# Shifting every operand by 192 bytes and staggering the split-weight buffers modulo 256 bytes

## The chip, the cores and the metric

The kernel runs on one core of one Trainium2 chip. The metric is the device time of one launch in microseconds. Three timed runs of the kernel before gave 2461.67 us in the median (2457.89 to 2467.87). One further execution was profiled; it took 2464.19 us by the same clock, of which 2462.4 us lie between its first and its last instruction (the span).

## What is computed

Two layers of a diffusion backbone over 256 latent tokens (and 256 context tokens in the first layer), model width 2048, feed-forward width 5632, all in float32. Cut to what matters here, with `h` the latent tokens:

```
for i in (0, 1):
    sh1, sc1, g1, sh2, sc2, g2 = ada_params(c, ada_w[i], ada_b[i])       # 6 x 2048 numbers
    a = modulate(h, sh1, sc1)                                            # h * (1 + scale) + shift
    y = na_mixer(a, ac, ...) if i == 0 else spatial_gating_mlp(a, ...)   # attention, then gMLP
    h = layer_norm(ALPHA * h + g1 * y, ln_g[i, 0], ln_b[i, 0])
    h = layer_norm(ALPHA * h + g2 * swiglu(modulate(h, sh2, sc2), ffn_w_in[i], ffn_w_out[i]),
                   ln_g[i, 1], ln_b[i, 1])
```

Nearly all the work is products of 256 (in layer 0's key and value projections 512) token rows with weight matrices that are read once from HBM.

## The kernel before, in words

**Products.** Every large product is made in three matmuls of type fp32r, which together stand for one float32 product: `mm3` (lines 87 to 90) multiplies the high part of the stationary operand with the high and the low part of the moving one, and the low part of the stationary one with the high part of the moving one. So each operand exists twice in SBUF, as a high and a low buffer. Each matmul has its own weight load (PEld in the profile). In the profile a group is named `out<-moving,stationary`: in `pod<-hwd,ghd` the weight piece `hwd` streams and the activation `ghd` is held.

**Weights.** They come in pieces of 128 partitions x 1024 float32 (4096 bytes in each partition, 512 KB). `prefetch` (lines 105 to 125) takes the next piece from one list that holds the order of the whole program, loads it into one of four `raw` buffers from SyncE's DMA queue (line 110), and splits it: `split_into` (lines 92 to 94) has ScalarE copy the raw piece to the high buffer (CAST, line 93) and VectorE subtract that copy from the raw piece into the low buffer (TENSOR_TENSOR, line 94). The high and low buffers stand in two places. The *narrow* ones, tags `hiA` and `loA`, three each in the pool `outer`, are used by all pieces of the attention part and by three of every five pieces afterwards. The *wide* ones, tags `hiB` and `loB`, two each in the pool `main`, take the other two of five (line 118). The last piece of each product goes to an `extra` tile.

**Activations.** In attention the modulated tokens are `ah` and `al`; in the feed-forward input products they are `f0h`/`f0l` (layer 0) and `f1h`/`f1l` (layer 1), in gMLP `m1h`/`m1l`. The feed-forward output product splits its activations as it goes, into `gh`/`gl` tiles of 256 columns (`ghd`, `gld`).

**Stages**, in us of the profiled span: 0 to 160 the first three heads' keys and values, with the first modulation computed beside them (`ap` tiles: dot products on TensorE, line 350, or on VectorE, line 337); to 660 attention and its output product; to 1165 the feed-forward input of layer 0 (`pg`, `pu`); to 1400 its output (`pod`); to 1730 gMLP; to 2450 the second feed-forward; then the last layer norm and the store. Beside the products VectorE computes later modulations (`ad`, line 152, `gate`, line 176) from weights that ScalarE's DMA queue loads into the four `ada` buffers.

**Addresses.** Tiles are laid in SBUF in the order in which pools and tags are opened, one after the other, each at the same byte address in all 128 partitions. Each starts at a multiple of 32 bytes. Three small tiles tagged `pad` (128, 128 and 64 bytes) stand in the pools `main`, `pw` and `gm`. What matters below is an address modulo 256, called the residue. Before the change, by the built program's table of addresses, every high, low, raw, `ada`, activation and gate buffer has residue 64; the `ap`, `xt`, `tmp` and `row` tiles of the first 160 us have 224; `sg`, `zs`, `gTb`, `w_s` and the broadcast rows have 192; `ident` has 0. Slices of these buffers start at multiples of 512 bytes, so that all 10,464 fp32r matmuls of the program read both operands from residue 64.

Of the kernel before, what the change touches and what calls it, by code (L numbers as in the profile page):

```python
# [11 lines left out]
F32 = mybir.dt.float32  # L12
F32R = mybir.dt.float32r
# [6 lines left out]
P = 128  # L20
# [21 lines left out]
FETCH = 3  # L42
BUSY = 0.3
DVE0 = 3
W0 = HK0 * P + 512
EARLY = tuple((3 + 4 * g + h, h, 4 * g) for g in range(3) for h in range(4))
EN = 4
# [4 lines left out]
def hybrid_kernel(ctx: ExitStack, tc: tile.TileContext, i, out):  # L52
# [3 lines left out]
    outer = ctx.enter_context(tc.tile_pool(name="outer", bufs=1))  # L56
# [10 lines left out]
    S.activation(c_col, c_col, AF.Silu)  # L67
    for t in (SC1, SC2):
        V.tensor_scalar(badj[:, :, t, :], badj[:, :, t, :], 1.0, None, ALU.add)
    lncol = outer.tile([P, 4, 2, KT], F32, tag="lncol", name="lncol")  # L70
    cols = outer.tile([P, 2, 6, KT], F32, tag="cols", name="cols")
    cols2 = outer.tile([P, 2, 6, KT], F32, tag="cols2", name="cols2")
# [14 lines left out]
    def mm3(ps, sh, sl, mh, ml, first, last, keep=lambda ins: ins):  # L87
        keep(T.matmul(ps, sh, mh, start=first, stop=False))  # L88
        keep(T.matmul(ps, sh, ml, start=False, stop=False))  # L89
        keep(T.matmul(ps, sl, mh, start=False, stop=last))  # L90

    def split_into(hi, lo, src):
        S.copy(hi, src)  # L93
        V.tensor_tensor(lo, src, hi.bitcast(F32), ALU.subtract)  # L94
# [5 lines left out]
    def enqueue(src, name, widths=(1024, 1024), extra=False):  # L100
        off = 0
        for n, w in enumerate(widths):
            queue.append((src[:, off : off + w], f"{name}_{off}", w, n if extra else None))
            off += w

    def prefetch(k):
        while len(ready) < k and queue:
            src, name, n, at = queue.pop(0)
            raw = outer.tile([P, 1024], F32, tag="raw", name=f"r{name}", bufs=RAW)
            (pin if pos["pin"] else lambda ins: ins)(nc.sync.dma_start(raw[:, :n], src))  # L110
            if at is not None:
                hi, lo = pos["extra"][:, 2 * at, :], pos["extra"][:, 2 * at + 1, :]
                split_into(hi, lo, raw)
                ready.append((hi, lo))
                continue
            m = pos["n"]
            pos["n"] += 1
            if pos["wide"] is not None and m % 5 > 2:
                pool, tag, bufs = pos["wide"], "B", 2
            else:  # L120
                pool, tag, bufs = outer, "A", 3
            hi = pool.tile([P, 1024], F32R, tag="hi" + tag, name=f"h{name}", bufs=bufs)
            lo = pool.tile([P, 1024], F32R, tag="lo" + tag, name=f"l{name}", bufs=bufs)
            split_into(hi[:, :n], lo[:, :n], raw[:, :n])
            ready.append((hi, lo))

    def piece():
        prefetch(1)
        got = ready.pop(0)
        prefetch(pos["bufs"] - 1)  # L130
        return got

    def take(k):
        prefetch(k)
        got = ready[:k]
        del ready[:k]
        return got
# [98 lines left out]
    for kt in range(KT):  # L236
        enqueue(i["w_kv0"][kt], f"kv{kt}", (W0,))
        for at, h, k0 in EARLY:
# [38 lines left out]
    with tc.tile_pool(name="attnX", bufs=1) as px, ExitStack() as late:  # L277
# [21 lines left out]
        with tc.tile_pool(name="st", bufs=1) as st:  # L299
# [3 lines left out]
            def load_st(src, name, n):  # L303
                pool, tag, bufs = slots[n % 4]
                r = pool.tile([P, 2048], F32, tag=tag, name=name, bufs=bufs)
                pin(nc.sync.dma_start(r, src))
                return r
# [3 lines left out]
            def fetch(kt):  # L311
                for t in range(2):
                    src = i["ada_s"][kt - DVE0] if t and kt >= DVE0 else i["ada_p"][kt, t]
                    held[kt, t] = load_st(src, f"ap{kt}{t}", 2 * kt + t)
# [18 lines left out]
            def dot_dve(kt, t):  # L333
                r = held.pop((kt, t))
                junk = outer.tile([P, D], BF16, tag="ada", name=f"junk{kt}", bufs=ADA)
                for n, (o, bc) in enumerate(((junk, cc_bc), (r, c_bc))):
                    V.scalar_tensor_tensor(
                        o, r, 1.0, bc, ALU.mult, ALU.mult, accum_out=raw_c[:, kt, 1 - n : 2 - n]
                    )
                V.tensor_scalar(mod[:, 1, kt, :], raw_c[:, kt, :], badj[:, 0, SH1, kt : kt + 1], None, ALU.add)  # L340

            def dot(kt, t):
                if t and kt >= DVE0:
                    return dot_dve(kt, t)
                if t == 0:
                    dps[kt] = stp_pool.tile([P, 512], F32, tag="a", name=f"aps{kt}")
                r = held.pop((kt, t))
                for kk in range(KT):
                    g = 32 * (kk % 4)
                    pin(T.matmul(  # L350
                        dps[kt][g : g + 32, t * P : (t + 1) * P], c_pad[:, kk, :], r[:, kk * P : (kk + 1) * P],
                        start=kk < 4, stop=kk >= KT - 4, tile_position=(0, g),
                    ))

            def gather(kt):
                ps = dps.pop(kt)
                ts = 1 if kt >= DVE0 else 2
                row = st.tile([P, 2 * P], F32, tag="row", name=f"row{kt}", bufs=1)
# [30 lines left out]
            for kt in range(KT):  # L389
                hi, lo = piece()  # L390
# [6 lines left out]
                def values(b):  # L397
                    c, tb = slice(HK0 * P, W0), slice(b * P, (b + 1) * P)
                    mm3(vps[b], ah[:, kt, tb], al[:, kt, tb], hi[:, c], lo[:, c], first, last, pin)
# [33 lines left out]
                for at, h, k0 in EARLY:  # L433
                    if at == kt:
                        h += HK0
                        hi, lo = piece()
# [537 lines left out]
def lay_out(x, c, ctx, c_ctx, ada_w, ada_b, ln_g, ln_b, na_w_qkv, na_w_o, na_rpb,  # L974
# [25 lines left out]
    )  # L1000
    a["ada_s"] = np.stack([aw[0, :, SH1, kt * P : (kt + 1) * P].T for kt in range(DVE0, KT)])
    wq, wk, wv = (na_w_qkv[0][:, n * D : (n + 1) * D] for n in range(3))
    w0 = np.concatenate([wk[:, : HK0 * P], wv[:, :512]], 1)
    a["w_kv0"] = w0.reshape(KT, P, W0)

# [34 lines left out]
```

## Time and profile before

| | |
|---|---|
| median of three runs | 2461.67 us |
| profiled execution, whole / span | 2464.19 / 2462.4 us |
| TensorE matmul busy | 2388.5 us, 97% |
| VectorE busy | 1753.7 us, 71% |
| ScalarE busy | 1120.5 us, 46% |
| GpSimd busy | 110.3 us, 4% |
| from HBM | 606.46 MB, 247 GB/s over the span |
| granted TensorE clock, mean | 0.991 |

Times are microseconds unless marked ns. A matmul's duration in a row (391 ns, say) is that of its passage through the array; the next one starts before it ends, so what a stream of matmuls costs is the distance between starts. L88 is line 88 of the kernel. A row of the lines view reads: line, engine, operation, out<-in, shapes, count | busy us, mean ns of one | idle time of the engine before them and who ended it. A row of a source view gives minimum, median and maximum of one instruction's duration.

### The profile page before, as it was taken

To read this page: it belongs to the slowest core of one execution; us is meant where nothing else is said; L and a number is where in the kernel's file an instruction comes from. 1 tells how busy PE (TensorE), PEld (TensorE's weight loads), DVE (VectorE), ACT (ScalarE), POOL (GpSimd) and SP (SyncE) were. 2 spreads that over 40 slices of the span, in tenths; PEclk is the share of its full clock that TensorE was granted. 3 is DMA by queue.
4 is the path that set the end of the run, shared out by engine and by line. 5 is a ranking of instruction groups with operands and counts; after the bars stand their busy time and mean duration, and the time that the engine had idled before them with its cause. 6 is when DMAs were issued, how large, how long until landed. Compare 5 with 4: busy or idle time off the path is not lost. (4 is left out here: it accounts for less than half of the span.)

```text
span 2462.4 us, 31266 instructions
## 1 busy us (share of the span) xinstructions
PE 2388.5 (97%) x11574; PEld 1979.4 (80%) x11574; DVE 1753.7 (71%) x2158; ACT 1120.5 (46%) x1534; POOL 110.3 (4%) x54
## 2 busy tenths in 40 slices
PE   7999999999999999999999999899999999999998
PEld 5788888888788888887888778777888888888886
DVE  4878877777887777666778778778755555566666
ACT  3344434335554444443455554445544444445453
POOL 0000200000010010000000010020100000020000
PEclk9999999999999999999999999999999999999999
DMA  9978787877578888887888767766567676766563
GB/s 358 346 248 266 254 288 260 273 253 246 188 241 284 293 280 299 284 290 275 280 290 283 247 208 263 241 210 196 199 229 229 226 227 225 230 198 190 178 211 131
DMA packets 167682, 610.63 MB, mean 248 GB/s; under 512 B 19076, under 2 KB 21572, under 8 KB 163172
## 3 DMA queue, kind: packets, MB, share of 16 engines
q1 hardware_dynamic: 120888, 440.64, 53.9%
q10 hardware_dynamic: 46512, 167.96, 19.9%
q8 instruction: 90, 1.47, 0.2%
q14 instruction: 64, 0.52, 0.1%
q0 software_dynamic: 128, 0.03, 0.0%
HBM read 606.46 MB, written 2.10 MB: 247 GB/s over the span
## 5 line engine op out<-in xcount | busy, mean ns | idle before, releaser
L93 ACT CAST hwf<-rwf 128x1024 fp32r<-128x1024 f32 x320 | 336.9, 1053 | 491.2 <-PE pu L90 206.0
L94 DVE TENSOR_TENSOR lwf<-rwf,hwf 128x1024 fp32r<-128x1024 f32 x320 | 404.3, 1277 | 173.8 <-ACT hwf L93 172.8
L152 DVE SCALAR_TENSOR_TENSOR ad<-ad,c_bc 128x1024 f32<-128x1024 f32 x192 | 234.0, 1222 | 168.9 <-DMA ad<-in_ada_t 168.3
L88 PE MATMUL pod<-hwd,ghd 128*128 128x512 f32 x684 | 267.3, 391 | 3.5 <-DVE sg L815 3.5
L90 PE MATMUL pod<-hwd,gld 128*128 128x512 f32 x684 | 266.5, 390 | 0.7 <-DVE gld L94 0.7
L89 PE MATMUL pod<-lwd,ghd 128*128 128x512 f32 x684 | 266.8, 390 | 0.0
L176 DVE SCALAR_TENSOR_TENSOR gate<-ag,c_col,gate 128x1024 f32<-128x1024 f32 x128 | 164.4, 1288 | 121.1 <-DMA ag<-in_ada_g 120.8
L94 DVE TENSOR_TENSOR lwd<-rwd,hwd 128x1024 fp32r<-128x1024 f32 x172 | 211.7, 1232 | 51.3 <-ACT hwd L93 51.0
L93 ACT CAST hwd<-rwd 128x1024 fp32r<-128x1024 f32 x172 | 180.3, 1049 | 33.3 <-PE pu L90 11.5
L88 PEld LDWEIGHTS pod<-hwd,ghd 128*128 128x128 f32 x684 | 128.7, 188 | 30.5 <-DVE sg L815 4.0
L90 PEld LDWEIGHTS pod<-hwd,gld 128*128 128x128 f32 x684 | 128.7, 188 | 28.1 <-DVE gld L94 1.2
L89 PEld LDWEIGHTS pod<-lwd,ghd 128*128 128x128 f32 x684 | 128.8, 188 | 26.6
L88 PE MATMUL pg<-hwf,f1h 128*128 128x512 f32 x320 | 126.4, 395 | 0.0
L88 PE MATMUL pg<-hwf,f0h 128*128 128x512 f32 x320 | 126.4, 395 | 0.0
L90 PE MATMUL pg<-hwf,f1l 128*128 128x512 f32 x320 | 124.7, 390 | 0.0
L90 PE MATMUL pg<-hwf,f0l 128*128 128x512 f32 x320 | 124.7, 390 | 0.0
L88 PE MATMUL pu<-hwf,f0h 128*128 128x512 f32 x320 | 124.5, 389 | 0.0
L89 PE MATMUL pu<-lwf,f0h 128*128 128x512 f32 x320 | 124.5, 389 | 0.0
L90 PE MATMUL pu<-hwf,f0l 128*128 128x512 f32 x320 | 124.5, 389 | 0.0
L88 PE MATMUL pu<-hwf,f1h 128*128 128x512 f32 x320 | 124.5, 389 | 0.0
L89 PE MATMUL pu<-lwf,f1h 128*128 128x512 f32 x320 | 124.5, 389 | 0.0
L90 PE MATMUL pu<-hwf,f1l 128*128 128x512 f32 x320 | 124.5, 389 | 0.0
(338 smaller groups left out, 5345.1 us busy)
## 6 DMA issues: line engine op xcount, KB each, us to landing
rwf<-in_w_in_t SPq DMA_DIRECT2D x320, 512.0 KB
ad<-in_ada_t ACTq DMA_DIRECT2D x192, 512.0 KB
rwd<-in_w_out SPq DMA_DIRECT2D x176, 512.0 KB
ag<-in_ada_g ACTq DMA_DIRECT2D x128, 512.0 KB
rwg<-in_w_gin SPq DMA_DIRECT2D x64, 512.0 KB
ap<-in_ada_p SPq DMA_DIRECT2D x19, 1024.0 KB
rwq<-in_w_q SPq DMA_DIRECT2D x32, 512.0 KB
rwo<-in_w_o SPq DMA_DIRECT2D x32, 512.0 KB
```

What stands on the lines that cost most here:

```text
L88: keep(T.matmul(ps, sh, mh, start=first, stop=False))
L89: keep(T.matmul(ps, sh, ml, start=False, stop=False))
L90: keep(T.matmul(ps, sl, mh, start=False, stop=last))
L93: S.copy(hi, src)
L94: V.tensor_tensor(lo, src, hi.bitcast(F32), ALU.subtract)
L152: V.scalar_tensor_tensor(r, r, 1.0, c_bc[:, half * 1024 : (half + 1) * 1024], ALU.mult, ALU.mult, accum_out=o[:, nt : nt + 1],)
L176: V.scalar_tensor_tensor(g, loaded.pop(key), c_col[:, kt, 0:1], g, ALU.mult, ALU.add)
```

## The change

Two edits; the arithmetic, the tiles' contents and the engines' programs stay as they are.

- A tile of 48 float32 (192 bytes in each partition) that nothing uses is put into `outer` ahead of `lncol`. Everything that is allocated after it moves up by at least 192 bytes.
- The narrow high buffers become 1024 + 24 elements long, the narrow low buffers 1024 + 40; only the first 1024 are used. Three buffers of a tag stand one after the other, so that their starts step by 96 bytes (high) and 160 bytes (low) modulo 256. What lies behind the six narrow buffers moves by 960 bytes in all.

```diff
+STEP_HI, STEP_LO = 24, 40
...
+    outer.tile([P, 48], F32, tag="pad", name="pad_outer")
     lncol = outer.tile([P, 4, 2, KT], F32, tag="lncol", name="lncol")
...
-            hi = pool.tile([P, 1024], F32R, tag="hi" + tag, name=f"h{name}", bufs=bufs)
-            lo = pool.tile([P, 1024], F32R, tag="lo" + tag, name=f"l{name}", bufs=bufs)
+            wh, wl = (1024 + STEP_HI, 1024 + STEP_LO) if tag == "A" else (1024, 1024)
+            hi = pool.tile([P, wh], F32R, tag="hi" + tag, name=f"h{name}", bufs=bufs)[:, :1024]
+            lo = pool.tile([P, wl], F32R, tag="lo" + tag, name=f"l{name}", bufs=bufs)[:, :1024]
             split_into(hi[:, :n], lo[:, :n], raw[:, :n])
```

Residues (byte address modulo 256) by the address tables of the two built programs:

```
buffers                                            before        after
narrow high (three)                                64 64 64      0 96 192
narrow low (three)                                 64 64 64      32 192 96
wide high and low, extra, raw, ada, ah, al,
  f0h/f0l, m1h/m1l, f1h/f1l, gh/gl, kh/kl, th/tl   64            0
ap (three of its four slots), xt, tmp, row         224           160
ap (the fourth slot: the gate buffer)              64            0
sg, zs, gTb, w_s, broadcast rows                   192           128
ident                                              0             0

fp32r matmuls by residues (moving, stationary)     before        after
512 columns, equal residues                        9504          4708 (0, 0)
512 columns, unequal                               0             4796
   of these with an operand at 32 or 96            0             2727
256 columns, equal residues                        960           352 (0, 0)
256 columns, unequal                               0             608
   of these with an operand at 32 or 96            0             360
```

The order of instructions on each engine, and what each waits for, is the same row by row in both programs.

## The prediction

> **What bounds the kernel now.** I read the page's busy times first, then the busy times by stage, then single matmuls in order of time, then the waits of TensorE, and last the groups of VectorE and ScalarE by shape.
>
> ```profile
> PE 2388.5 (97%) x11574; PEld 1979.4 (80%) x11574; DVE 1753.7 (71%) x2158; ACT 1120.5 (46%) x1534; POOL 110.3 (4%) x54
> ```
>
> TensorE is busy for 2388.5 of 2462.4 us; 73.9 us are left. The same by stage (columns: length, busy us of PE, PEld, DVE, ACT, POOL, granted clock, DMA share, GB/s):
>
> ```profile
> 0.00:100.00 100.00, 84.19 (x725) 65.34 (x726) 61.08 (x84) 37.49 (x61) 5.24 (x8) 0.97 0.94 353
> 100.00:660.00 560.00, 541.47 (x3003) 463.94 (x3002) 436.27 (x633) 244.49 (x391) 15.23 (x3) 0.99 0.78 261
> 700.00:1165.00 465.00, 465.00 (x2092) 384.93 (x2090) 331.97 (x352) 197.56 (x212) 20.45 (x7) 1.00 0.85 287
> 1400.00:1730.00 330.00, 310.22 (x1355) 250.55 (x1354) 256.73 (x312) 165.84 (x237) 35.44 (x21) 0.97 0.66 220
> 1730.00:2450.00 720.00, 719.59 (x3222) 595.23 (x3221) 442.62 (x450) 326.58 (x404) 27.86 (x11) 1.00 0.65 209
> 2450.00:2463.00 13.00, 0.67 (x3) 0.21 (x2) 8.78 (x15) 0.29 (x1) 0.00 (x0) 0.63 0.31 120
> ```
>
> In the two feed-forward stages (465 and 720 us) TensorE never waits; 0.4 us are lost in 1185. All idle time lies in the first 100 us (15.8), attention (18.5), gMLP (19.8), the 13 us behind the last product, and a rest at the edges. So time can come from two places only: the distance between matmuls in a stream, or these edges.
>
> The distance, from 197 matmuls of 512 columns in a row (first and last shown) and 27 of 256 columns:
>
> ```profile
> 1199.74 0.39 PE L90 MATMUL pod<-hwd,gld 128*128 128x512 f32 x1
> ...
> 1244.17 0.39 PE L88 MATMUL pod<-hwd,ghd 128*128 128x512 f32 x1
> ```
>
> ```profile
> 165.83 0.28 PE L90 MATMUL qps<-ah,lwq 128*128 128x256 f32 x1
> ...
> 168.95 0.28 PE L89 MATMUL qps<-al,hwq 128*128 128x256 f32 x1
> ```
>
> 44.43 us / 196 = 226.7 ns, and 3.12 us / 26 = 120.0 ns. The 256 columns more cost 106.7 ns, so 512 cost 213.3, and 13.3 ns of each matmul do not depend on its width. That fixed 13.3 ns is the one part of a stream's time that addresses might touch.
>
> **The pads and the shift.** No instruction is added, removed or moved, no wait is added, and each transfer has the same size. What remains is whether an access takes another time at another address. I go through those who access SBUF.
>
> *TensorE.* Rows of single matmuls by line, minimum/median/maximum in ns:
>
> ```profile
> L88 PE MATMUL pu<-hwf,f0h x320: 389/389/389, 740.6 to 1161.6; 128*128 128x512 f32 x160
> L88 PE MATMUL pu<-hwf,f1h x320: 389/389/389, 1788.1 to 2209.2; 128*128 128x512 f32 x160
> ```
>
> In 640 matmuls none is a nanosecond longer than another, while ScalarE writes, VectorE reads and writes and the DMA queues fill other buffers at the same residue 64 all the time (DVE 71%, DMA share 0.85 in that stage). Three of five of those weight pieces stand in narrow buffers and two in wide ones, which differ in where they lie but not in residue. So the other engines' accesses cost TensorE nothing that staggering could give back: term 0.0 us. The bounds: all of the 13.3 ns goes away for the pairs that become unequal (first rival), or reads that start 32 bytes off cost more (second rival).
>
> The Trainium skill speaks against any such gain: "SBUF — State Buffer", section "Who interferes with whom", holds that only the port pair shared by VectorE and GpSimd causes contention, and that TensorE and ScalarE wait on nobody. By that rule the term would be 0.0 too, for every residue; the 640 equal durations agree with it for the other engines, but no row here shows it for TensorE's own two reads, which always stood at one residue.
>
> *VectorE.*
>
> ```profile
> L94 DVE TENSOR_TENSOR lwf<-rwf,hwf x320: 1209/1224/10147, 710.4 to 2197.6; 128x1024 fp32r<-128x1024 f32 x160
> L94 DVE TENSOR_TENSOR gld<-gTb,ghd x109: 416/423/426, 1205.5 to 2432.6; 128x256 fp32r<-128x256 f32 x109
> L94 DVE TENSOR_TENSOR al<-tmp,ah x16: 691/693/693, 15.7 to 152.7; 128x512 fp32r<-128x512 f32 x16
> L94 DVE TENSOR_TENSOR lwe<-rwe,hwe x12: 683/689/689, 42.6 to 146.1; 128x512 fp32r<-128x512 f32 x12
> L152 DVE SCALAR_TENSOR_TENSOR ad<-ad,c_bc 128x1024 f32<-128x1024 f32 x192 | 234.0, 1222 | 168.9 <-DMA ad<-in_ada_t 168.3
> L337 DVE SCALAR_TENSOR_TENSOR junk<-ap,oT x13: 2280/2282/2283, 36.9 to 143.9; 128x2048 bf16<-128x2048 f32 x13
> ```
>
> With all operands at 64, (1224 - 423) / 768 = 1.043 ns per element. L337 reads `ap` at residue 224, an odd multiple of 32 like the new 32 and 96: (2282 - 1222) / 1024 = 1.035. Its 13 instructions, six of them at 224 and seven at 64 in the gate buffer, lie within 3 ns. `al<-tmp,ah` reads at 224 and takes 4 ns more than `lwe<-rwe,hwe`, whose operands all stand at 64. So the term per split lies between -13 ns (median to minimum of `lwf`) and +4 ns. The narrow buffers take some 500 pieces, so VectorE changes by between -6.5 and +2 us over the run, under the cover of TensorE's stream in all stages without idle time: 0.0 us on the path. Without that cover, at the edges, where a twentieth of the pieces stands (some 25), it would be 0.3 us at most. The maximum of 10147 ns in the first row is a split that stood behind a GpSimd broadcast or reduction, and addresses do not change which instructions meet.
>
> *ScalarE.*
>
> ```profile
> L93 ACT CAST hwf<-rwf x320: 1037/1055/1060, 708.9 to 2196.5; 128x1024 fp32r<-128x1024 f32 x160
> L93 ACT CAST ghd<-gTb x109: 395/407/409, 1204.0 to 2431.4; 128x256 fp32r<-128x256 f32 x109
> ```
>
> (1055 - 407) / 768 = 0.844 ns per element with everything at 64 except `gTb`, which is at 192; durations spread over 23 ns. At most -18 ns a piece, hidden in the same way (ACT 46% busy): 0.0 us.
>
> *DMA.* Its targets `raw` and `ada` go from 64 to 0 modulo 256. The stage that it fills most is the first: share 0.94 at 353 GB/s, thus 376 GB/s per fully busy share, and there most bytes go to `ap` and `xt` at 224. In the stage at 0.85 and 287 GB/s, 338 per share, all go to residue 64. The stage with the odder residues is the faster one (its transfers are larger), so no handicap of a residue is to be seen. What quicker transfers could give back is bounded by TensorE's waits that a DMA ended:
>
> ```profile
> PE aps L350 <- DMA ap<-in_ada_p: 8.1, 2, 7.6
> PE pt L552 <- ACT p L542: 13.4, 7, 5.0
> PE gu L89 <- DVE lwg L94: 3.3, 1, 3.3
> PE vps L89 <- DVE lwv L94: 2.1, 2, 1.7
> ```
>
> 7.6 of the 8.1 us are the first load after the start, a latency. The longest other waits are for a softmax chain (`pt`) and for VectorE's split of a late piece (`gu`, `vps`). I take 0.0 us, with bounds of 0 and -16 us (all idle time of the first 100 us).
>
> The Trainium skill has a rule for this too: "DMA: Bandwidth & Descriptors", section "How a descriptor splits into AXI transactions", says that a transaction must start at a multiple of 256 bytes, so that a descriptor that begins elsewhere wastes beats. By its account of 32-byte beats, 4096 bytes from residue 64 would take 130 beats and from residue 0 128; my estimate from that page is 1.5% of the raw transfers, about 1 us of the stage that DMA fills. No row here separates targets at 0 from targets at 64 at this size.
>
> *Sum:* 2464.2 + 0.0 (TensorE) + 0.0 (VectorE, ScalarE) + 0.0 (DMA) = 2464 us for a profiled execution. The profiled execution stands 2.5 us above the median of 2461.67, so the forecast for the median is 2461 us, rounded. Its own range is 2449 to 2474, half a per cent to either side; half a per cent, 12.3 us, is also about what a measurement of this kernel can tell from no change.
>
> **Rivals.**
>
> *A, faster: TensorE's two reads collide when they stand at one residue.* For it: all 10,464 fp32r matmuls read both operands from residue 64, and all carry the same 13.3 ns, so the trace cannot tell a fixed cost from a collision that always happens. Against it: the loads read 512 bytes and the streams 1024 or 2048, and a collision that is paid anew as both walk on should grow with the overlap or scatter, where 640 rows show one value. After the change 4796 matmuls of 512 columns and 608 of 256 have unequal residues: 5404 x 13.3 ns = 71.9 us, thus 2392 us profiled and 2390 in the median. Chance 0.13.
>
> The Trainium skill gives this rival a figure: "TensorE: Matmul & The Clock Gate", section "Back-to-back issue gap", has N/2.4 + 2.5 ns for the gap, 215.8 ns at 512 columns. The trace disagrees with it by 10.9 ns a matmul; if the unequal pairs fell to the page's gap, 58.9 us would go by my estimate.
>
> *B, slower: reads that start at 32 modulo 64 cost TensorE more.* Before, no fp32r matmul reads from there; afterwards 2727 of 512 columns and 360 of 256 do (narrow buffers at 32 and 96). TensorE has no cover, so each nanosecond counts in full. As a price I take what the stream pays where its feed is uneven, in the first stage:
>
> ```profile
> L89 PE MATMUL vps<-lkv,ah 128*128 128x512 f32 x64 | 25.7, 401 | 0.0
> L90 PE MATMUL eps<-ah,lwe 128*128 128x512 f32 x48 | 18.7, 389 | 0.0
> ```
>
> 401 - 389 = 12 ns; 3087 x 12 = 37.0 us, thus 2501 profiled and 2499 in the median. It decides from 12.3 us / 3087 = 4.0 ns a matmul. Against it: VectorE's rate at residue 224 above; TensorE's fp32 products from `ap` at 224 run too, but none at another residue stands beside them in the full clock. Chance 0.11.
>
> *C, faster at the edges.* The waits of the stages that are not filled shrink because raw pieces land and are split sooner. All such idle time is 15.8 + 18.5 + 19.8 = 54.1 us; half of it would be 27 us, 2434 in the median. For it: `gu` and `vps` wait for splits. Against it: the longest wait for a split is 3.3 us, and neither the split nor the DMA shows a cost of residue 64. Chance 0.09. Edges that grow by over half a per cent get 0.04, for waits that fall differently.
>
> **How the numbers follow.** No change 0.63; faster 0.13 + 0.09 = 0.22; slower 0.11 + 0.04 = 0.15. The range goes from 2430, which takes in C and leaves out A in full (about 0.12), to 2485, which takes in B up to 24 us (3087 x 7.8 ns) and leaves out some 0.07. That is just under 2 in 10.
>
> **What would show it.** Right: a stream of `pod` matmuls is still 226.7 ns apart, pieces in narrow and in wide buffers alike; 465 us of PE in the first feed-forward stage with 2092 matmuls; `lwf` near 1224 and `hwf` near 1055 ns; idle time of TensorE near 74 us. A shows itself as two distances within one stage, 213 ns for low and two of three high narrow pieces and 227 for wide ones; B as narrow pieces at 32 and 96 that are slower than the one at 192; C as a smaller idle time with the same distance. I am wrong if the distance differs anywhere from 226.7 in a stream, or if the median lies outside 2449 to 2474.

## The result, and the profile after

| | before | after |
|---|---|---|
| median of four runs each | 2463.82 us | 2490.77 us |
| ratio, 95% interval | | 1.011 (1.0082 to 1.0139) |
| span of the profiled execution | 2462.4 us | 2484.4 us |
| granted TensorE clock, mean | 0.991 | 0.993 |

(A fourth run of the kernel before has joined the three of the opening section, which moves its median from 2461.67 to 2463.82.) The kernel became 1.1% slower, where no change had been forecast. 2490.77 lies above the range's upper end of 2485. The clock did not cause it: it was granted slightly higher.

The page's busy times of the kernel after:

```profile
PE 2415.8 (97%) x11574; PEld 1974.8 (79%) x11574; DVE 1756.0 (71%) x2158; ACT 1118.6 (45%) x1534; POOL 109.5 (4%) x54
```

TensorE is busy for 27.3 us longer (2388.5 before) with the same 11,574 matmuls. Its idle time is 2484.4 - 2415.8 = 68.6 us, 5.3 less than before. So all of the 22.0 us by which the span grew, and more, came into TensorE's stream. By stage (length, busy PE, PEld, DVE, ACT, POOL, clock, DMA share, GB/s):

```profile
700.00:1165.00 465.00, 465.00 (x2061) 379.33 (x2060) 329.25 (x350) 195.81 (x211) 21.95 (x8) 1.00 0.83 280
1730.00:2450.00 720.00, 718.64 (x3173) 585.16 (x3173) 431.86 (x435) 329.76 (x415) 27.23 (x11) 1.00 0.65 209
```

TensorE still never waits in the first of these stages and hardly in the second, and the clock is full. Yet 2061 matmuls fit where 2092 did, and 3173 where 3222 did: 1.5% fewer. VectorE and ScalarE do less per microsecond as well, because they follow TensorE. Their own durations did not move, by the groups of the long weight pieces on ScalarE and VectorE:

```profile
L95 ACT CAST hwf<-rwf 128x1024 fp32r<-128x1024 f32 x320 | 335.9, 1050 | 502.7 <-PE pu L92 229.0
L96 DVE TENSOR_TENSOR lwf<-rwf,hwf 128x1024 fp32r<-128x1024 f32 x320 | 404.0, 1272 | 192.4 <-ACT hwf L95 191.4
```

The row of single matmuls that had read 389/389/389 (minimum, median, maximum in ns):

```profile
L90 PE MATMUL pu<-hwf,f0h x320: 387/392/400, 747.6 to 1175.2; 128*128 128x512 f32 x160
```

It now scatters over 13 ns. Where the scatter sits is seen in the starts of `pod` matmuls in the timeline, at the borders of four weight pieces of 12 matmuls each. The first two pieces lie in narrow buffers, the next two in wide ones:

```profile
1251.28 0.39 PE L90 MATMUL pod<-hwd,ghd 128*128 128x512 f32 x1
...
1254.07 0.40 PE L90 MATMUL pod<-hwd,ghd 128*128 128x512 f32 x1
...
1256.85 0.39 PE L90 MATMUL pod<-hwd,ghd 128*128 128x512 f32 x1
...
1259.61 0.39 PE L90 MATMUL pod<-hwd,ghd 128*128 128x512 f32 x1
...
1262.33 0.39 PE L90 MATMUL pod<-hwd,ghd 128*128 128x512 f32 x1
```

Per matmul that is 2.79 us / 12 = 232.5 ns and 231.7 ns in the narrow pieces, 230.0 in the first wide one and 226.7 in the second. Only the second wide piece runs at the distance of before. The starts in nanoseconds show how (distance to the next start):

```
narrow: 234 232 225 236 236 236 228 236 229 226 233 232
narrow: 237 231 234 234 226 231 237 225 233 234 227 231
wide:   232 234 236 224 231 235 229 232 231 227 226 227
wide:   227 226 227 226.7 on average from here to the next narrow piece
```

The wide pieces have equal residues for weights and activations (0 and 0), yet it takes nine matmuls behind a narrow piece until they run evenly. The mean over all pieces of `pg`, `pu` and `pod` is 231.7 ns in narrow pieces, 230.3 in the first wide piece behind one and 226.7 to 227.1 in the second. Per group of five pieces that is (3 x 5.0 + 3.6 + 0.4) / 5 = 3.8 ns a matmul, and 7872 matmuls of the large weight products x 3.8 = 29.9 us. The 256-column products of the query weights got a little faster (the unequal ones 117.7 ns apart in the mean, 119.7 before), which takes 608 x 2.0 = 1.2 us off.

The sum, 28.7 us, lies near the 27.3 measured, but in part by chance: it leaves out the attention's 1632 matmuls of 512 columns, 1188 of which became unequal too, and takes streams as unbroken that are not. Counted in the two traces, each matmul up to the start of the next or to its own end, the large weight products take 23.3 us more (22.2 of it in `pg`, `pu` and `pod`), the attention's 512-column products 6.7 us more, the 256-column ones 3.7 us less and all else 0.9 us more: 27.3 us. Not all of the 3.7 us is owed to residues, as the 256-column products of the pad alone (below), which stay equal, also take 1.7 us less.

### The profile page after: what moved, and what is told of

Same layout as the page of the kernel before. It is cut to its first block, busy times and chain, and to the rows that moved or that the text cites. A ratio compares the mean times of both kernels' runs of the same rounds, so it can differ in the third digit from the quotient of the medians.

```text
span 2484.4 us, 31266 instructions
## 1 busy us (share of the span) xinstructions
PE 2415.8 (97%) x11574; PEld 1974.8 (79%) x11574; DVE 1756.0 (71%) x2158; ACT 1118.6 (45%) x1534; POOL 109.5 (4%) x54
## 5 line engine op out<-in xcount | busy, mean ns | idle before, releaser
L95 ACT CAST hwf<-rwf 128x1024 fp32r<-128x1024 f32 x320 | 335.9, 1050 | 502.7 <-PE pu L92 229.0
L96 DVE TENSOR_TENSOR lwf<-rwf,hwf 128x1024 fp32r<-128x1024 f32 x320 | 404.0, 1272 | 192.4 <-ACT hwf L95 191.4
L96 DVE TENSOR_TENSOR lwd<-rwd,hwd 128x1024 fp32r<-128x1024 f32 x172 | 211.5, 1231 | 51.3 <-ACT hwd L95 50.9
```

## Experiments

Four theories were to be told apart. T1: a 512-column fp32r matmul costs more when its moving operand (the weights) and its stationary operand (the activations) stand at unequal residues modulo 256. T2: reads that start at 32 modulo 64 cost more (rival B of the prediction). T3: the move from residue 64 to 0 costs, whatever the steps. T4: it is the weight buffers' inequality among each other that costs. Pads in the diffs are counted in float32 elements of 4 bytes. The first three diffs and that of the steps alone are against the kernel after, the others against the kernel before or, for TensorE alone, a program of its own.

The measure used throughout is the window from 1800 to 2200 us, in which TensorE never waits: how many matmuls fit into 400 us. The kernel before and the kernel after:

```profile
1800.00:2200.00 400.00, 400.00 (x1802) 331.35 (x1801) 225.27 (x188) 170.05 (x181) 12.77 (x1) 1.00 0.69 224
```

```profile
1800.00:2200.00 400.00, 400.00 (x1774) 326.24 (x1773) 223.47 (x186) 165.97 (x176) 12.78 (x1) 1.00 0.68 220
```

**The pad alone.** Every operand moves from 64 to 0 and all stay equal.

```diff
-STEP_HI, STEP_LO = 24, 40
+STEP_HI, STEP_LO = 0, 0
```

> Only the 192-byte pad: every high, low, raw and activation buffer stands at residue 0, all fp32r pairs equal again. Theory T1 (what costs is the staggering: a moving operand whose residue differs from the stationary one's): as the kernel before, 2464 us (+-6), streams at 226.7 ns in every piece. Theory T2 (starts at 32 modulo 64 cost): nothing starts there, 2464 us. Theory T3 (the shift from residue 64 to 0 costs, since pieces at (0, 0) in wide buffers also scatter): slow as the changed kernel, about 2490 us, with distances of 226 to 236 ns.

Measured: 2466.48 against 2465.93 us for the kernel before, ratio 1.0007 (0.9988 to 1.0026).

```profile
1800.00:2200.00 400.00, 400.00 (x1799) 330.89 (x1798) 225.33 (x188) 169.60 (x180) 12.77 (x1) 1.00 0.68 223
```

1799 matmuls, as before. T3 falls: the shift costs nothing.

**All operands at 96.** A pad of 32 bytes and no steps, so that every read starts at 32 modulo 64.

```diff
-STEP_HI, STEP_LO = 24, 40
+STEP_HI, STEP_LO = 0, 0
...
-    outer.tile([P, 48], F32, tag="pad", name="pad_outer")
+    outer.tile([P, 8], F32, tag="pad", name="pad_outer")
```

> A pad of 32 bytes and no staggering: every large buffer stands at residue 96, thus at 32 modulo 64, and all fp32r pairs are equal. T1: as before, 2464 us, 226.7 ns. T2: all 10,464 fp32r matmuls start 32 bytes off; at the 5 ns that narrow pieces lost, 2464 + 52 = 2516 us, 231.7 ns. T3 (only residue 64 is good): slow, 2490 us or more.

Measured: 2459.11 us, ratio 0.9983 (0.9963 to 1.0003).

```profile
L90 PE MATMUL pu<-hwf,f0h x320: 389/389/389, 745.4 to 1166.8; 128*128 128x512 f32 x160
```

Again all 320 matmuls are equal, at a residue that rival B had priced at 12 ns a matmul, and 1800 matmuls fit the window. T2 falls, and with it any cost of the residue as such.

**Steps of 64 and 192 bytes.** All starts are multiples of 64, but unequal: high at 0, 64, 128 and low at 192, 128, 64.

```diff
-STEP_HI, STEP_LO = 24, 40
+STEP_HI, STEP_LO = 16, 48
```

> The pad, and steps of 64 and 192 bytes instead of 96 and 160: narrow high buffers at 0, 64, 128, narrow low ones at 192, 128, 64, all else at 0. All start at multiples of 64, but five of six narrow buffers are unequal to the stationary operand. T1: narrow pieces at about 231.7 ns, as in the changed kernel, 2485 to 2495 us. T2: 226.7 ns and 2464 us. T3: slow like e1 would be.

Measured: 2486.8 us, ratio 1.0106 (1.0077 to 1.0134).

```profile
1800.00:2200.00 400.00, 400.00 (x1777) 327.18 (x1776) 223.34 (x186) 165.14 (x175) 12.78 (x1) 1.00 0.67 220
```

Nothing starts at 32 modulo 64, and the time is that of the change. T1 and T4 are left.

**The steps alone.** The change without its pad.

```diff
-    outer.tile([P, 48], F32, tag="pad", name="pad_outer")
```

> Only the lengthened narrow buffers, without the 192-byte pad: wide buffers and activations stay at residue 64, narrow high ones at 64, 160, 0, narrow low ones at 96, 0, 160. T1 (unequal residues of moving and stationary operand cost): slow as the changed kernel, 2485 to 2495 us, narrow pieces at 231.7 ns. If pad and steps cost only together: 2464 us.

Measured: 2493.1 against 2465.78 us, ratio 1.0118 (1.0082 to 1.0155).

```profile
1800.00:2200.00 400.00, 400.00 (x1773) 326.24 (x1773) 222.67 (x190) 167.18 (x177) 8.41 (x1) 1.00 0.68 220
```

The lengthened buffers do all of it. In the profiled executions TensorE is busy for 2388.5, 2385.0 and 2387.3 us where all pairs are equal (before, pad alone, all at 96), and for 2415.8, 2416.2 and 2416.9 us in the three kernels with steps.

**The activations moved, the weights not.** Pads ahead of and behind the activations' and the feed-forward product's tiles put these at 160; all weight buffers stay at 64. By the address table of the built program 7836 of the 7872 matmuls of the large weight products become unequal (36 at the end of the last product read activations from another buffer), and no weight buffer differs from another.

```diff
+            outer.tile([P, 24], F32, tag="pad_g", name="pad_g")
...
+            outer.tile([P, 40], F32, tag="pad_g2", name="pad_g2")
...
+        if "a" not in padded:
+            main.tile([P, 24], F32, tag="pad_a", name="pad_a")
...
+            main.tile([P, 40], F32, tag="pad_a2", name="pad_a2")
...
```

> No staggering of weight buffers at all (all at 64 as before); instead the activations of the output products, the feed-forward and gMLP move by 96 bytes to residue 160, so that 7872 matmuls of 512 columns have a difference of 160 bytes, in wide and narrow pieces alike. T1: every one of these loses, by 5.0 ns (as narrow pieces did) to 7.6 ns (the pair stream with this difference took 234.25 ns): 2464 + 39 to + 60 = 2503 to 2524 us. A rival T4 (what costs is that consecutive moving operands, or the buffers that the engines fill, differ among each other): 2464 us, 226.7 ns, since all weight buffers are equal here.

Measured: 2510.47 us, ratio 1.0182 (1.0152 to 1.0212), the slowest of all.

```profile
1800.00:2200.00 400.00, 400.00 (x1744) 322.29 (x1743) 215.27 (x189) 165.15 (x176) 0.00 (x0) 1.00 0.67 220
```

```profile
PE 2439.4 (97%) x11574; PEld 1982.1 (79%) x11574; DVE 1760.0 (70%) x2158; ACT 1119.8 (45%) x1534; POOL 107.6 (4%) x54
```

TensorE is busy for 50.9 us longer than before, 6.5 ns for each of the 7836. In `pg`, `pu` and `pod` the matmuls stand 234.2 ns apart, in narrow and wide pieces alike. T4 falls. T1 is left, and the cost grows with the number of unequal matmuls.

**TensorE alone, pair by pair.** A program without the model (it only copies its input to the output): 66 streams of 36 fp32r matmuls each (the expectation counts 76), and no other engine at work during a stream. Moving and stationary operand are read from offsets of choice in one buffer each.

```diff
+    T.matmul(ps[:, 0:n], a[:, s : s + P], w[:, m : m + n], start=k == 0, stop=k == N - 1)
```

> This kernel leaves out the whole model: it copies x to the output and runs 76 streams of 36 fp32r matmuls, each stream with moving and stationary slices of two tiles at chosen byte offsets (steps of 8 or 16 bytes over 256; equal offsets; 256 columns; two moving offsets in turn), TensorE alone, 36 matmuls then a pause. It gives the distance between matmuls by pair of residues. T1: 226.7 ns where the difference of residues is 0, whatever the common one, and about 232 ns elsewhere. T2: 226.7 ns for every moving offset that is a multiple of 64, 232 ns at 32 modulo 64. T3: 226.7 nowhere but with both at 64 (not among the offsets of equal residue 0). A cost that comes from the other engines' traffic: 226.7 ns everywhere.

Measured, some streams in the timeline (start, length of the stream): the moving operand 8, 72, 112 and 192 bytes ahead, then equal offsets of 32, 64, 96, 128 and 192 bytes.

```profile
22.74 8.65 PE L49 MATMUL ps<-w,a 128*128 128x512 f32 x36 [0.78 <-DVE sink L52]
...
97.99 8.72 PE L49 MATMUL ps<-w,a 128*128 128x512 f32 x36 [0.78 <-DVE sink L52]
...
145.15 8.43 PE L49 MATMUL ps<-w,a 128*128 128x512 f32 x36 [0.79 <-DVE sink L52]
...
239.39 8.67 PE L49 MATMUL ps<-w,a 128*128 128x512 f32 x36 [0.78 <-DVE sink L52]
...
465.52 8.44 PE L49 MATMUL ps<-w,a 128*128 128x512 f32 x36 [0.78 <-DVE sink L52]
474.74 8.46 PE L49 MATMUL ps<-w,a 128*128 128x512 f32 x36 [0.78 <-DVE sink L52]
483.99 8.47 PE L49 MATMUL ps<-w,a 128*128 128x512 f32 x36 [0.78 <-DVE sink L52]
493.24 8.47 PE L49 MATMUL ps<-w,a 128*128 128x512 f32 x36 [0.78 <-DVE sink L52]
502.49 8.46 PE L49 MATMUL ps<-w,a 128*128 128x512 f32 x36 [0.78 <-DVE sink L52]
```

The five equal pairs take 8.44 to 8.47 us, and the unequal ones shown here up to 0.28 us more, 8 ns for each of the 35 distances. The exception is 112 bytes ahead. From the starts of single matmuls, mean distance over the last 24 of a stream, by how far the moving operand stands ahead (the stream at 0 is the first of the program and settles only within these 24, at 226.7):

```
bytes ahead  0      8      16     32     64     96     112    128    160    192    240
ns           227.1  233.3  231.7  233.3  228.9  233.3  226.7  232.1  234.2  233.3  236.7
```

So no other engine is needed: TensorE's own two reads decide. 160 bytes ahead, the difference of the kernel with the activations moved, takes the same 234.2 ns here as there. An equal pair first scatters and then settles. At 96 bytes its distances are 335, 229, 234, 236, 224, 231, 235, 229, 232, 231, 227, 226, 227 and 226.7 from there on, nearly number for number the settling of the wide piece above. One equal pair, 16 bytes off on both sides, did not settle (231.1).

**The activations 144 bytes on.** The map says that the moving operand may stand 112 bytes ahead without cost. Here weights stay at 64 and the activations of `pg`, `pu`, `gu` and `gv` move to 208.

```diff
+ACT_AT = 36
...
+            main.tile([P, KT * NT + 64], F32R, tag="act" + p, name=name + p)[:, ACT_AT : ACT_AT + KT * NT]
...
```

> As e6, but only the activations of the feed-forward input and gMLP move, by 144 bytes, so that the moving operand stands 112 bytes above the stationary one modulo 256; the pair streams had 226.67 ns at 112 bytes, without a settling time. T1 in the strict form (any unequal pair costs): pg, pu, gu and gv matmuls at 231 ns or more, some 4700 of them, 2464 + 20 = 2484 us or more. T1 as the pair map has it (certain differences lock, 0 and 112 among them): 226.7 ns in these groups, 2464 us.

Measured: 2489.95 us, ratio 1.0097 (1.0069 to 1.0125).

```profile
L89 PE MATMUL pu<-hwf,f0h x320: 394/394/400, 742.6 to 1175.5; 128*128 128x512 f32 x160
```

```profile
1800.00:2200.00 400.00, 400.00 (x1754) 322.63 (x1753) 221.07 (x185) 163.53 (x174) 12.77 (x1) 1.00 0.66 217
```

The map failed here: these products stand 233.3 ns apart, while `pod` and the others that were left equal keep 226 to 227. That products slow down exactly where they became unequal speaks for T1. That 112 bytes did not come free was open until the last run.

**Widths and types.** TensorE alone again, without the model, streams of 60: fp32r at four widths, bf16, and plain fp32.

```diff
-    w = pool.tile([P, 2048], F32R, tag="w", name="w")
+    w = {k: pool.tile([P, 2048], t, tag="w" + k, name="w" + k) for k, t in (("r", F32R), ("b", BF16), ("f", F32))}
```

> Leaves out the model like e4 and runs streams of 60 matmuls of TensorE alone: fp32r with 512 columns at differences of 0, 112, 256, 512 and 1024 bytes and at equal offsets; fp32r with 256 columns at 16 differences, and with 128 and 384; bf16 and plain fp32 at several differences. If the cost has a period of 256 bytes: 226.7 ns at 256, 512 and 1024. If the floor is N + 32 cycles of 2.4 GHz: 384 columns take 173.3 ns and 256 never less than 120.0; if it is N times 17/16: 170.0 ns, and 113.3 at some differences (e4 had 113.33 at 192 bytes). If the cost comes of two streams of 4-byte words at full rate: bf16 (half the bytes) and fp32 (two cycles a column, by its 215 ns for 256 columns) show one distance at every difference.

Measured: 512 columns 256 bytes ahead and equal at 112 bytes; 256 columns at 0, at 192 bytes ahead and with the stationary operand 64 ahead; bf16 at 0 and 48 bytes; fp32 at 64 bytes.

```profile
42.38 13.89 PE L55 MATMUL ps<-wr,ar 128*128 128x512 f32 x60 [0.78 <-DVE sink L58]
...
101.18 14.14 PE L55 MATMUL ps<-wr,ar 128*128 128x512 f32 x60 [0.78 <-DVE sink L58]
...
130.78 7.45 PE L55 MATMUL ps<-wr,ar 128*128 128x256 f32 x60 [0.78 <-DVE sink L58]
...
225.33 7.09 PE L55 MATMUL ps<-wr,ar 128*128 128x256 f32 x60 [0.52 <-DVE sink L58]
...
256.55 7.09 PE L55 MATMUL ps<-wr,ar 128*128 128x256 f32 x60 [0.52 <-DVE sink L58]
...
356.34 13.11 PE L55 MATMUL ps<-wb,ab 128*128 128x512 bf16 x60 [0.51 <-DVE sink L58]
...
384.12 13.11 PE L55 MATMUL ps<-wb,ab 128*128 128x512 bf16 x60 [0.78 <-DVE sink L58]
...
452.54 26.17 PE L55 MATMUL ps<-wf,af 128*128 128x256 f32 x120 [0.52 <-DVE sink L58]
```

256 bytes ahead is as good as equal (13.89 us, 226.7 ns). Equal starts at 112 bytes, 16 modulo 32, are not (14.14 us, 231.1 ns). At 256 columns the order turns round: equal starts take 120.0 ns, 192 bytes ahead 113.3. bf16 (215.8 ns at 512 columns) and plain fp32 (215.8 ns at 256, for each of the two records that a matmul leaves) take one time at all offsets tried, and so does fp32r at 128 columns (111.7). The sensitivity was seen in fp32r from 256 columns on only.

**Only the 256-column products unequal.** A version that takes what the run before offers: the query weights and the attention's value parts (`vh`, `vl`), which are the stationary operands of the 256-column products, start 64 bytes further on, and all other operands of fp32r matmuls stay at 64. To make room, the `bias` buffers go from two to one.

```diff
+Q_AT = 16
...
+            at = Q_AT if name.startswith("wq") else 0
+            hi = pool.tile([P, long], F32R, tag="hi" + tag, name=f"h{name}", bufs=bufs)[:, at : at + 1024]
...
-                    bias = pb.tile([P, 6 * GW], F32, tag="bias", name=f"bias{h}", bufs=2)
+                    bias = pb.tile([P, 6 * GW], F32, tag="bias", name=f"bias{h}", bufs=1)
...
+                        pb.tile([P, 16], F32, tag="pad_v", name="pad_v")
```

> The kernel before with one use of the pair map: only the 960 matmuls of 256 columns get unequal residues. Query weights are put 64 bytes into their narrow buffers (which become 256 bytes longer, so that all else stays at 64), the attention's value parts stand 64 bytes further, and one buffer instead of two holds the bias. All 9504 matmuls of 512 columns stay equal. The map had 113.33 ns for 256 columns at this pair of offsets and 120.00 at equal ones. T1 with the map: qps and o matmuls at 113 to 117 ns, 960 x 3 to 6.7 ns = 3 to 6 us less, thus 2458 to 2461 us, a ratio of 0.9975 to 0.999. If the streams of some 24 matmuls are too short to settle: 2464 us, distances scattered between 113 and 123 ns.

Measured: 2462.58 against 2467.1 us, ratio 0.9981 (0.9964 to 0.9997).

```profile
PE 2383.9 (97%) x11574; PEld 1974.7 (80%) x11574; DVE 1754.5 (71%) x2158; ACT 1120.6 (45%) x1534; POOL 109.4 (4%) x54
```

The 27 distances of a stream that is 120.0 ns apart in the kernel before (the `qps` stream of the prediction) come to 117.8 ns:

```profile
165.80 0.28 PE L91 MATMUL qps<-ah,lwq 128*128 128x256 f32 x1
...
168.98 0.28 PE L91 MATMUL qps<-ah,lwq 128*128 128x256 f32 x1
```

Over all of them the 256-column products stand 116.2 ns apart in the mean (119.7 before), the 512-column ones still 226.7. That makes 960 x 3.5 = 3.4 us. The shorter distance is shown; that it made the kernel faster is not. The ratio lies at the edge of what was measured, the kernel with all operands at 96, where no pair is unequal, came out as low (0.9983), and the 4.6 us by which TensorE is less busy here are little more than the 3.5 us of the pad alone.

**Where 112 bytes ahead holds.** TensorE alone, without the model, 34 streams of 60: from seven starts of the stationary operand, once with one buffer each and once with high and low buffers in the kernel's turn.

```diff
+            wi, ai = ((0, 0), (0, 1), (1, 0))[k % 3] if kind == 3 else (0, 0)
```

> TensorE alone again, the model left out: 34 streams of 60 fp32r matmuls of 512 columns. Half of them read one moving and one stationary buffer; half take high and low buffers in the kernel's turn (high-high, low moving, low stationary) with the weight slice walking on by 512 bytes. Open since the run with the activations at 144 more: there the moving operand stood 112 bytes ahead of the stationary one, which by the first stream run should take 226.7 ns, and took 231. Theory T5 (the stationary start must also be a multiple of 32 bytes; there it was 208 = 16 modulo 32): 112 bytes ahead takes 226.7 from stationary starts 0, 32, 64 and 192, and 230 or more from 16, 80 and 208, with one buffer and in turn alike; equal starts take 226.7 at 0, 32 and 192 and 230 or more at 16, 48, 80, 144 and 208. Theory T6 (the turn of the buffers breaks it): with one buffer 112 ahead takes 226.7 from every start, in turn 230 or more from every start, while equal starts at 0, 32 and 192 stay at 226.7 in turn, as in the kernel. 96 and 32 bytes ahead in turn: about 233 by both, as in the kernel with the activations at 96 more.

Measured, with one buffer: 112 bytes ahead from stationary starts 16, 32 and 192; equal at 0. In turn: 112 ahead from 16, equal at 0 and at 32.

```profile
27.00 13.87 PE L49 MATMUL ps<-w,a 128*128 128x512 f32 x60 [0.78 <-DVE sink L52]
41.65 14.14 PE L49 MATMUL ps<-w,a 128*128 128x512 f32 x60 [0.78 <-DVE sink L52]
...
86.54 13.87 PE L49 MATMUL ps<-w,a 128*128 128x512 f32 x60 [0.78 <-DVE sink L52]
...
116.25 13.94 PE L49 MATMUL ps<-w,a 128*128 128x512 f32 x60 [0.78 <-DVE sink L52]
...
279.69 14.27 PE L49 MATMUL ps<-w,a 128*128 128x512 f32 x60 [0.78 <-DVE sink L52]
...
369.60 13.89 PE L49 MATMUL ps<-w,a 128*128 128x512 f32 x60 [0.79 <-DVE sink L52]
...
399.32 13.92 PE L49 MATMUL ps<-w,a 128*128 128x512 f32 x60 [0.78 <-DVE sink L52]
```

Both theories fall in half. With one buffer 112 ahead takes 226.7 ns from 16 and 192 only, and 231.1 to 233.3 from 0, 32, 64, 80 and 208; from 0 it had taken 226.7 in both earlier stream runs. So one and the same pair has two steady cycles. Which of them it falls into may depend on how the stream begins (here it was the first of the program, whose first seven distances are 426 ns or more); no run varied the beginning alone. In turn it took 231.1 to 233.3 from all seven starts, and from 208 the 233.3 ns that the kernel with the activations at 208 showed. Equal starts at 0, 32 and 192 settle at 226.7 with one buffer and in turn alike, behind every beginning seen; equal starts at 16, 48, 80, 144 and 208 never do (230.0 to 233.3).

## Why the prediction was wrong

**What bounds the kernel: right.** Time could come only from the distance between matmuls or from the edges, and the distance is where it came from. That the 13.3 ns are "the one part of a stream's time that addresses might touch" was right in place and wrong in sign: it is no fixed part that could only shrink, since unequal pairs of 512 columns mostly take longer than 226.7 ns, up to 236.7. Nor is it one part for all widths: two widths had given 13.3 ns + 0.417 ns a column, which would make 66.7 ns at 128 columns, and the streams took 111.7.

**The step that failed: the TensorE term of 0.0 us.** It rested on 640 matmuls of one duration and on the sentence that other engines' accesses cost TensorE nothing that staggering could give back. The sentence was true, and beside the point. All 640 stood at one pair of residues, and equal residues at a multiple of 32 bytes are the very setting in which a stream settles to one distance; the row showed that state, not insensitivity. Moved to residue 96 together, it still reads 389/389/389; moved apart, it scatters and costs 5.0 ns a matmul in narrow pieces. Measured, the term is +27.3 us in the profiled execution. The prediction did see that no row showed TensorE's own two reads at unequal residues, and still let them cost something only where a read starts at 32 modulo 64; the bound for plain inequality on the slower side was missing.

The rule of the Trainium skill that was quoted there says the same 0.0: by "SBUF — State Buffer", section "Who interferes with whom", TensorE waits on nobody, and for the other engines the runs agree (the streams with TensorE alone show the kernel's distances). That TensorE is disturbed by its own pair of reads, by 2 to 10 ns beside 226.7, the rule does not say; here the measurement decides.

**VectorE, ScalarE, DMA at 0.0: right.** In the mean `hwf` took 1050 ns where 1053 stood and `lwf` 1272 where 1277 stood, and TensorE's idle time behind VectorE's splits of weight pieces did not grow (6.8 us in all, 7.0 before). The DMA rate fell a little in the first feed-forward stage, as the weights are used up more slowly (280 GB/s, 287 before). What a DMA target's residue costs, which the prediction could not tell, is seen in the pad alone and in the kernel at 96: the 4096-byte packets of the weight queue took 159 ns in the median at residues 64, 0 and 96 (mean 199.3, 197.8 and 197.4). The 1.5% that the prediction had estimated between 64 and 0 would have been 2.4 ns of 159.

**Rival A: the right place, the wrong sign.** TensorE's two reads do act on each other by their residues. At 512 columns equal residues are the good case, by 2 to 10 ns; only at 256 columns are unequal ones mostly faster, by up to 6.7 ns, and 608 of those gave back about a microsecond.

**Rival B: near in time, wrong in mechanism.** Its 2499 us lies closest to the result, by luck: it charged 3087 matmuls with 12 ns, where 4796 were unequal and lost less each. Its sign even appeared: in the kernel after the change the mean distances of `pu` are, by the weights' residue,

```
weights at   96 high       96 low   32 low   192 high      192 low   0 high        0 low
ns           235.6, 232.1  234.4    232.9    230.8, 230.4  227.3     228.8, 229.8  228.8
```

(the second number of a pair is that of the low activations). But with every operand at 96 the kernel is not slower, and with multiples of 64 alone it is just as slow. A look at the trace of the changed kernel could have confirmed B; only a kernel in which the residue changes and the difference does not could refute it. B's price, 12 ns from `vps` in the first stage, was also not what it was taken for: streams there are interrupted after every six matmuls and settle again each time (distances of 236, 229, 232 and 231 ns behind the break), as the streams of TensorE alone do in their first ten matmuls.

**Rival C: did not come.** Idle time fell by 5.3 us, not by 27.

**Left open:** why fp32r streams settle at equal residues and at which other differences, and what within TensorE has the two cycles. The runs show the distances, not the parts that collide.

## What to carry to other kernels

Where fp32r matmuls of 512 columns run back to back, allot their moving and stationary operands at one residue modulo 256 bytes, at a multiple of 32 (0, 32, 64, 96, 128 and 192 were tried); pads and odd buffer lengths can cost 1 to 2% of a kernel that TensorE bounds. A duration that never varies at one setting says nothing of another setting: before a term is set to zero, ask whether the trace has ever shown the thing that the change alters. To test a staggering, move all buffers together once, and apart once.

## What the runs showed of the hardware

- fp32r streams with a weight load for each matmul have steady cycles. At 512 columns the fast one is 226.7 ns; slower ones run at 228.3 to 236.7, often in a pattern of three (225, 231, 238 for 112 bytes ahead).
- A disturbed stream of equal pairs comes back to 226.7 ns within about ten matmuls (335, 229, 234, 236 and so on to 227). Short pieces at another residue cost the piece behind them as well: 3.6 ns a matmul in the first wide piece.
- The widths do not follow one line: 111.7 ns at 128 columns, 113.3 to 120.0 at 256, 173.3 to 176.7 at 384, 226.7 to 236.7 at 512. "TensorE: Matmul & The Clock Gate" of the Trainium skill, section "Back-to-back issue gap", gives N/2.4 + 2.5 as the gap of an isolated matmul, 215.8 ns at 512 columns. Streams of bf16 stand just that far apart here (215.8 ns), streams of fp32r further (226.7 at best).
